# Twelve of the 22 row chunks of a down projection as seven block products in place of eight, placed inside the up stage

## The chip, the cores and the metric

The kernel runs on one core of a Trainium2 chip. The metric is the time of one execution on the device in microseconds. TensorE (PE in the profile, PEld for its weight loads) multiplies; VectorE (DVE) and ScalarE (ACT) do the elementwise work; GpSimd (POOL) does little here; SyncE (SP) issues nearly all transfers. The engines run side by side, each through its own instructions in order, and wait for each other through semaphores.

## What is computed

Two encoder layers on 512 tokens of width 1024. Each adds to the residual `x` a mixture of three attention branches, and then a feed-forward part. Only the second is touched:

```python
def conv_ffn(h, w_up, conv_w, conv_b, w_down):      # D_FF = 2816, D_MODEL = 1024
    u = h @ w_up
    C = u.shape[-1]
    u = lax.conv_general_dilated(u, conv_w[:, None, :].astype(u.dtype), window_strides=(1,),
                                 padding=((CONV_W // 2, CONV_W // 2),),
                                 dimension_numbers=('NWC', 'WIO', 'NWC'),
                                 feature_group_count=C) + conv_b
    a, g = jnp.split(u, 2, axis=-1)
    return (jax.nn.gelu(g) * a) @ w_down

for l in range(DEPTH):                              # DEPTH = 2
    ...
    h = rmsnorm(x, norm2_g[l])
    x = x + conv_ffn(h, w_up[l], conv_w[l], conv_b[l], w_down[l])
return rmsnorm(x, final_g)
```

## The kernel before

Everything is held transposed: features on the 128 partitions, the 512 tokens along a row. `x` is eight tiles of 128x512 (`self.x[k]`, two of which carry other names in the trace). A product of full float32 accuracy is made of three matmuls in the format fp32r: weight and data are each split into a high part (a rounded copy, ACT, L153) and a low part (the remainder, one subtraction on DVE, L154), and `mm3` (L162 to L169) adds high times high, high weight times low data, low weight times high data into one PSUM bank.

Weights: `self.specs` lists every block of weights in the order of use. `fetch` loads each into one of three buffers `raw` by a DMA on SP's queue and splits it into `whi` and `wlo`, three buffers each. `weights(spec)`, called just ahead of a block's matmuls, lets the loads run to two blocks ahead and the splits too; a pair of split buffers is free again when the matmuls of the block three places earlier are done.

The up stage (`do_up`, `conv`) walks 22 value chunks f and their 22 gate chunks in turns: 24 matmuls of 512 columns make one chunk in one of eight PSUM banks; DVE scales it by the norm (`u`), ACT and DVE apply the three taps of the convolution (`c`, L906 to L908), a gate chunk goes through Gelu and is multiplied with its value chunk, and the product is split into the pair `ff` of its chunk. The down stage (`do_down`) then has two groups of four output tiles. A group walks the 22 chunks of `ff` in pieces of 8, 8 and 6: for each piece and each of the four output tiles one block of weights, 24, 24 and 18 matmuls, into that tile's bank (`ps_g`). After the last piece DVE adds the bank to `x[k]`, once for each tile (L944; in three tiles of the last layer L941 and L978), and the next norm begins. The last three tiles of the last layer are multiplied in `finish`, two of them in halves of 256 tokens.

The order on PE and SP is the order of the code (`manual_schedule`). On ACT and DVE a scheduler sets the order when the program is built, from priorities: a split runs 300 places ahead (`PRIO`). Engines are held apart by semaphores that count their instructions; a PSUM tile is watched as a whole.

Of the kernel before, what the change touches and what calls it, by code (L numbers as in the profile page):

```python
# [10 lines left out]
F32 = mybir.dt.float32  # L11
# [3 lines left out]
ALU = mybir.AluOpType  # L15
# [21 lines left out]
LAT = (0, 1, 2, 3)  # L37
ATTN, ATTN_PRIO = ("mr", "ms", "mt", "mp", "ns", "nt", "np", "gs", "gt", "gp"), 100
RAWB, WB, GZB, PRIO = 3, 3, 5, 300
ROWS = (slice(0, 64), slice(64, 128))  # L40
HALVES = (ROWS, ROWS[::-1])

# [17 lines left out]
class Trunk:  # L60
# [5 lines left out]
    def __init__(self, ctx, tc, d):  # L66
        self.tc, self.nc, self.d, self.ctx = tc, tc.nc, d, ctx
        nc = self.nc
        self.small = ctx.enter_context(tc.tile_pool(name="small", bufs=1))
        self.const = ctx.enter_context(tc.tile_pool(name="const", bufs=1))  # L70
        self.wp = ctx.enter_context(tc.tile_pool(name="wp", bufs=1))
        self.psum = ctx.enter_context(tc.tile_pool(name="psum", bufs=1, space=bass.MemoryType.PSUM))
        self.groups, self.turn = {}, {}
        c = self.const
        x0 = c.tile([P, S + NPC], F32, name="x0")
        self.x = [x0[:, :S]] + [c.tile([P, S], F32, name=f"x{k}") for k in range(1, KD)]
        self.par = [x0[:, S:], self.small.tile([P, NPC], F32, name="par1")]
        self.early = c.tile([P, P], F32, tag="acc", name="early")
        nc.vector.memset(self.early, 1.0)
        self.idf = c.tile([P, P], F32, name="idf")  # L80
        make_identity(nc, self.idf)
        cst = self.small.tile([P, 6], F32, name="cst")
        self.neghalf, self.ones = cst[:, 0:4], cst[:, 4:5]
        nc.vector.memset(self.neghalf, -0.5)
        nc.vector.memset(self.ones, 1.0)
        self.warm = cst[:, 5:6]
        nc.scalar.activation(self.warm, self.ones, AF.Exp)
        self.specs, self.raws, self.parts, self.used = [], [], [], 0
        self.plans = [self.schedule(l) for l in range(L)]
        for s, W in self.plans:  # L90
            self.specs += [w for item in s for w in W.get(item, ())]
        nc.sync.dma_start(x0[:, :S + PC_CW], d["x0"])
        self.fetch(1, 0)
        for k in range(1, 5):
            nc.sync.dma_start(self.x[k], d["xT"][k * P:(k + 1) * P, :])
            self.fetch(min(k + 1, 3), 0)
        self.gmask = self.small.tile([P, 3 * P], BF16, name="gmask")
# [12 lines left out]


    def fetch(self, n_raw, n_split):
        nc = self.nc
        while len(self.raws) < min(n_raw, len(self.specs)):
            w, r0, nk, c0, cw = self.specs[len(self.raws)]
            raw = self.wp.tile([P, 1024], F32, tag="raw", name="raw", bufs=RAWB)
            for q, a, b in ((nc.sync, 0, cw),) if self.raws else ((nc.scalar, 0, P), (nc.sync, P, cw)):
                q.dma_start(raw[:, :nk * cw].rearrange("p (k c) -> p k c", c=cw)[:, :, a:b],
                            w[r0:r0 + nk * P, c0 + a:c0 + b].rearrange("(k p) c -> p k c", p=P))
            self.raws.append(raw)  # L120
        while len(self.parts) < min(n_split, len(self.raws)):
            i = len(self.parts)
            w, r0, nk, c0, cw = self.specs[i]
            hi = self.wp.tile([P, 1024], F32R, tag="whi", name="whi", bufs=WB)
            lo = self.wp.tile([P, 1024], F32R, tag="wlo", name="wlo", bufs=WB)
            if cw == 64:
                both = hi[:].rearrange("p (k c) -> p k c", c=P)
                with self.tc.high_priority(offset=PRIO if self.prio else 0):
                    self.split(both[:, :, 0:64], both[:, :, 64:P],
                               self.raws[i][:, :nk * cw].rearrange("p (k c) -> p k c", c=cw))  # L130
                self.parts.append((both, both))
                continue
            with self.tc.high_priority(offset=PRIO if self.prio else 0):
                if i:
                    self.split(hi[:, :nk * cw], lo[:, :nk * cw], self.raws[i][:, :nk * cw])
                else:
                    for cp, c in ((nc.vector.tensor_copy, slice(0, P)), (nc.scalar.copy, slice(P, 4 * P))):
                        cp(hi[:, c], self.raws[i][:, c])
            self.parts.append(tuple(t[:, :nk * cw].rearrange("p (k c) -> p k c", c=cw) for t in (hi, lo)))

    def weights(self, spec):
        i = self.used
        assert self.specs[i][1:] == spec[1:]
        self.fetch(i + RAWB, i + WB)
        self.used += 1
        wh, wl = self.parts[i]
        return [(wh[:, k, :], wl[:, k, :]) for k in range(spec[2])]


    def split(self, hi, lo, src, scale=None):  # L150
# [123 lines left out]
    def schedule(self, l):  # L274
# [30 lines left out]
        W["up"] = halves(d["w_up"][l], [f * P for f in ups[:4]])  # L305
        for f in ups[4:]:
            W["up", f] = [(d["w_up"][l], 0, KD, f * P, P)]
        for g in range(2):
            W["down", g] = [(d["w_down"][l], k0 * P, nk, (4 * g + m) * P, P)
                            for k0, nk in ((0, 8), (8, 8), (16, 6)) for m in range(4)]  # L310

        gate = iter([("gate", b, m) for b in (1, 0, 2) for m in range(8)]).__next__
        s = ["mla_open", "lat", "qr", "lat4", "rs_q", "kr", gate(), "rs_k", ("qn", 0), ("v", 0), ("v", 1), "rb_k"]
# [16 lines left out]
            s += [gate(), ("br", 2, m)]  # L330
        s += [("br", 2, 7)]
        s += ["out"] + [("out", m) for m in range(4, KD)]
        s += ["up"] + [("up", f) for f in ups[4:]]
        s += [("down", 0), ("down", 1)]
        return s, W

# [551 lines left out]
    def do_up(self, fi=None):  # L888
        if fi is None:
            self.banks(g=[2, 3, 4, 5], r=[6], d=[7, 0, 1, 2, 3, 4, 5, 6])  # L890
            self.fps, self.fp = self.open("ff")
            self.ff = []
            ups = [0, NF, 1, NF + 1]
            conv = lambda *js: [self.conv(ups[j], self.gbank[j]) for j in js]
            self.group(self.W["up"], self.h, {(0, 1): lambda: (self.norm_sums(), self.norm_spread()), (1, 0): lambda: conv(0), (1, 1): lambda: conv(1),
                                              (1, 2): lambda: conv(2), (1, 3): lambda: conv(3)})
        else:
            self.conv(fi, self.dense(self.spec(), self.h))

    def conv(self, fi, ps):  # L900
        nc, pr = self.nc, self.pr
        u = self.fp.tile([P, S], F32, tag="u", name="u", bufs=2)
        self.mul(u, ps, self.rb)
        c = self.fp.tile([P, S], F32, tag="c", name="c", bufs=3)
        cw = pr[:, PC_CW + 3 * fi:PC_CW + 3 * fi + 3]
        nc.scalar.activation(c, u, AF.Identity, bias=pr[:, PC_CB + fi:PC_CB + fi + 1], scale=cw[:, 1:2])  # L906
        nc.vector.scalar_tensor_tensor(c[:, 1:], u[:, :S - 1], cw[:, 0:1], c[:, 1:], ALU.mult, ALU.add)
        nc.vector.scalar_tensor_tensor(c[:, :S - 1], u[:, 1:], cw[:, 2:3], c[:, :S - 1], ALU.mult, ALU.add)  # L908
        if fi < NF:
            self.ca = c  # L910
            return
        nc.scalar.activation(c, c, AF.Gelu_apprx_tanh)
        self.mul(self.ca, self.ca, c)
        f = fi - NF
        pair = [self.fp.tile([P, S], F32R, tag=f"f{n}{f}", name="ff") for n in "hl"]
        self.split(*pair, self.ca)
        self.ff.append(pair)

    def do_down(self, g):
        nc = self.nc  # L920
# [12 lines left out]
        for i, spec in enumerate(self.W["down", g]):  # L933
            m, k0, nk = i % 4, spec[1] // P, spec[2]
            if last and (g, k0, m) == (1, 16, 1):
                self.finish([self.weights(sp) for sp in self.W["down", 1][i:]], self.ff[k0:k0 + nk])
                break
            tail = last and g == 1 and m > 0
            self.mm3(ps[m], self.weights(spec), self.ff[k0:k0 + nk], k0 == 0, k0 == (8 if tail else 16))
            if tail and k0 == 8:  # L940
                nc.vector.tensor_add(self.x[4 + m], self.x[4 + m], ps[m])  # L941
            if k0 == 16:
                k = 4 * g + m
# [6 lines left out]
                else:  # L950
                    self.norm_piece(k, self.par[self.l + 1][:, PC_G1:PC_G1 + 8])
        if g == 1:
            self.fps.close()

    def finish(self, sts, mv):
# [7 lines left out]
        for k in range(5, KD):  # L963
            self.xg.append(self.const.tile([P, S], F32, tag=f"hh{k}", name="xg"))
        sq = [self.const.tile([P, S], F32, tag=f"hl{k}", name="sq") for k in range(5, KD)]
        outs = [self.fp.tile([P, 2, S], F32, tag="o", name="o", bufs=3) for _ in range(3)]
        outs.append([self.const.tile([P, S], F32, tag=t, name="o") for t in ("hl3", "hl4")])
        rts = self.small.tile([P, 4], F32, tag="rt", name="rts", bufs=3)
        eps = self.small.tile([P, 4], F32, tag="ms", name="eps", bufs=2)
# [6 lines left out]
        def add(m, ts):  # L976
            x = self.x[4 + m][:, ts]
            nc.vector.tensor_add(x, x, ps[m][:, ts])  # L978
            nc.scalar.activation(sq[m - 1][:, ts], x, AF.Square)
# [139 lines left out]
```

## Time and profile before

| | us |
|---|---|
| median of three timed runs | 1689.85 (1689.12 to 1689.95) |
| the profiled execution | 1688.89 |
| its span, first to last instruction | 1687.1 |
| PE busy | 1678.7, 8466 matmuls |
| PE weight loads busy | 1388.2 |
| DVE busy | 1119.5 |
| ACT busy | 832.5 |

A row of the timeline gives the start and the duration of an instruction, or of several alike (x3), both in microseconds; in a group row the numbers behind the first bar are the busy time and the mean duration in nanoseconds. Matmuls run into each other: each row's duration holds the time in which its last results drain while the next matmul already runs. What a matmul costs in a full stream is therefore the distance between starts, not its duration. The same holds, less strongly, for DVE and ACT.

### The profile page before, as it was taken

Reading aid. Unit: us, or ns where it says so; the run is one execution under the profiler, and the core shown is the slowest. Engines: PE = TensorE matmul, PEld = TensorE weight load, DVE = VectorE, ACT = ScalarE, POOL = GpSimd, SP = SyncE. Lnnn points to the kernel's source line nnn. Section 1 sums busy time; section 2 is a strip of 40 time slices with the busy share of each in tenths; the row PEclk is TensorE's granted clock in tenths of the full one; section 3 lists DMA queues with packets and bytes.
Section 4 is the critical chain, followed back from the end, with each engine's and each line's share of the span. In section 5 each row is a group of like instructions: output and inputs, shape, how many; then the busy total and the mean of one; then the engine's idle time right before and its main releaser. Section 6 shows DMA issues by size and latency. Waiting matters only on the chain.

```text
span 1687.1 us, 22130 instructions
## 1 busy us (share of the span) xinstructions
PE 1678.7 (100%) x8466; PEld 1388.2 (82%) x8466; DVE 1119.5 (66%) x1845; ACT 832.5 (49%) x1461; POOL 51.8 (3%) x107
## 2 busy tenths in 40 slices
PE   9999999999999999999999999999999999999998
PEld 8888888888888888888887888888888888888887
DVE  7677866787558777734367687667866587777234
ACT  7664445775435444423266554457744444444232
POOL 1110000000000000000011100000000000000000
PEclk9999999999999999999999999999999999999999
DMA  6233323222334333323233323332223333333231
GB/s 186 67 98 90 89 77 88 81 63 81 108 87 118 99 91 99 100 87 103 79 97 82 91 82 94 82 88 63 69 83 106 106 102 99 100 99 91 86 106 69
DMA packets 289401, 155.44 MB, mean 92 GB/s; under 512 B 8880, under 2 KB 285376, under 8 KB 289296
## 3 DMA queue, kind: packets, MB, share of 16 engines
q1 hardware_dynamic: 286752, 148.88, 30.8%
q0 software_dynamic: 2256, 4.83, 0.9%
q8 instruction: 66, 1.08, 0.3%
q14 instruction: 39, 0.32, 0.1%
q10 hardware_dynamic: 288, 0.33, 0.1%
HBM read 151.89 MB, written 2.10 MB: 91 GB/s over the span
## 4 chain that ended last, share of the span: by engine, by line
PE 97%; DVE 2%; ACT 0%; issue 0%; ACTq 0%
PE ps_ring L167 13%; PE ps_ring L168 12%; PE ps_ring L169 12%; PE ps_d L169 11%; PE ps_d L168 11%; PE ps_d L167 11%; PE ps_g L168 7%; PE ps_g L167 7%; PE ps_g L169 7%; PE ps_ring L247 2%; PE ps_ring L234 1%; PE ps_g L267 1%; PE ps_ring L702 1%; PE ps_ring L857 1%; PE ps_ring L856 1%; DVE wlo L154 1%
## 5 line engine op out<-in xcount | busy, mean ns | idle before, releaser
L153 ACT CAST whi<-raw 128x1024 fp32r<-128x1024 f32 (+4 forms) x339 | 301.0, 888 | 589.0 <-PE ps_g L168 192.3
L154 DVE TENSOR_TENSOR wlo<-raw,whi 128x1024 fp32r<-128x1024 f32 (+4 forms) x337 | 344.4, 1022 | 183.7 <-ACT whi L153 183.1
L169 PE MATMUL ps_d<-hh,wlo 128*128 128x512 f32 x685 | 266.5, 389 | 0.0
L168 PE MATMUL ps_d<-hl,whi 128*128 128x512 f32 x685 | 266.5, 389 | 0.0
L167 PE MATMUL ps_d<-hh,whi 128*128 128x512 f32 x685 | 266.5, 389 | 0.0
L167 PE MATMUL ps_ring<-hh,whi 128*128 128x512 f32 x600 | 235.3, 392 | 0.5 <-DVE pt L674 0.5
L169 PE MATMUL ps_ring<-hh,wlo 128*128 128x512 f32 x600 | 233.8, 390 | 0.0
L168 PE MATMUL ps_ring<-hl,whi 128*128 128x512 f32 x600 | 233.6, 389 | 0.0
L168 PEld LDWEIGHTS ps_d<-hl,whi 128*128 128x128 f32 x685 | 128.6, 188 | 27.0
L167 PEld LDWEIGHTS ps_d<-hh,whi 128*128 128x128 f32 x685 | 128.6, 188 | 26.8
L169 PEld LDWEIGHTS ps_d<-hh,wlo 128*128 128x128 f32 x685 | 128.6, 188 | 26.6 <-DVE wlo L154 0.2
L167 PEld LDWEIGHTS ps_ring<-hh,whi 128*128 128x128 f32 x600 | 112.7, 188 | 24.4 <-DVE pt L674 0.9
L169 PEld LDWEIGHTS ps_ring<-hh,wlo 128*128 128x128 f32 x600 | 112.6, 188 | 23.8
L168 PEld LDWEIGHTS ps_ring<-hl,whi 128*128 128x128 f32 x600 | 112.6, 188 | 23.1
L168 PE MATMUL ps_g<-ff,whi 128*128 128x512 f32 x334 | 129.9, 389 | 0.0
L169 PE MATMUL ps_g<-ff,wlo 128*128 128x512 f32 x334 | 129.9, 389 | 0.0
L167 PE MATMUL ps_g<-ff,whi 128*128 128x512 f32 x334 | 129.9, 389 | 0.0
L160 DVE TENSOR_TENSOR u<-ps_d,rb 128x512 f32<-128x512 f32 x80 | 55.2, 690 | 63.2 <-PE ps_d L169 63.2
L160 DVE TENSOR_TENSOR gz<-ps_ring,rb 128x512 f32<-128x512 f32 x44 | 30.4, 690 | 78.1 <-PE ps_ring L169 78.1
L167 PEld LDWEIGHTS ps_g<-ff,whi 128*128 128x128 f32 x334 | 62.7, 188 | 13.1
L169 PEld LDWEIGHTS ps_g<-ff,wlo 128*128 128x128 f32 x334 | 62.7, 188 | 13.1
L168 PEld LDWEIGHTS ps_g<-ff,whi 128*128 128x128 f32 x334 | 62.7, 188 | 12.9
(331 smaller groups left out, 2859.5 us busy)
## 6 DMA issues: line engine op xcount, KB each, us to landing
raw<-in_w_in_dram SPq DMA_DIRECT2D x86, 512.0 KB, 3.9
raw<-in_w_up_dram SPq DMA_DIRECT2D x80, 512.0 KB, 3.8
raw<-in_w_down_dram SPq DMA_DIRECT2D x32, 512.0 KB, 3.9
raw<-in_w_down_dram SPq DMA_DIRECT2D x16, 384.0 KB, 3.4
raw<-in_w_in_dram SPq DMA_DIRECT2D x17, 256.0 KB, 2.9
raw<-in_w_br_mla_dram SPq DMA_DIRECT2D x16, 256.0 KB, 2.7
raw<-in_w_br_na_dram SPq DMA_DIRECT2D x16, 256.0 KB, 2.7
raw<-in_w_br_gqa_dram SPq DMA_DIRECT2D x16, 256.0 KB, 2.8
```

Source lines behind the costliest of these rows:

```text
L153: nc.scalar.copy(hi, src)
L154: nc.vector.tensor_sub(lo, src, r32(hi))
L160: self.nc.vector.tensor_tensor(out, a, b, ALU.mult)
L167: mm(ps, sh, mh, start=first and k == 0, stop=False)
L168: mm(ps, sh, ml, start=False, stop=False)
L169: mm(ps, sl, mh, start=False, stop=last and k == n - 1)
L234: self.nc.tensor.transpose(out[i][:, n * 64:n * 64 + 64], block[q], self.idf[q, q])
L247: self.nc.tensor.matmul(out, st[a], mv[b], start=first and t == 0, stop=last and t == 2)
L267: self.nc.tensor.matmul(self.gbank[j], w[:, j * P:(j + 1) * P], m, start=n + t == 0, stop=False)
L702: nc.tensor.matmul(pq[:, qs], self.vs[p][:, ch, j, :], pm[:].rearrange("p (k c) -> p k c", c=P)[:, ks], start=i == 0 and m == 0, stop=i == ...
L856: nc.tensor.matmul(po, self.gvs[:, k0 + kb, g, :], ph, start=kb == 0, stop=False)
L857: nc.tensor.matmul(po, self.gvs[:, k0 + kb, g, :], pl, start=False, stop=kb == nk - 1)
```

## The change

Per layer, the first 12 of the 22 chunks (6 pairs of chunks, `NP = 6`) are multiplied by the scheme of seven block products in place of eight (Strassen's, in Winograd's form). A unit takes two neighbouring output tiles (`m`, `m + 1`), the even and the odd chunk of each pair, and the two halves of the tokens: 2 x 2 blocks of weights, 2 x 2 blocks of data. Seven combinations of weight blocks (`ORDER`, each 128x768: six blocks of 128 columns) meet seven combinations of data blocks (`B11` to `T4`, each 256 tokens wide). Each of the seven is an item of 6 x 3 = 18 matmuls of 256 columns. There are four units in each layer, so 28 items and 504 matmuls.

- Data: `sum_operands` puts the gated product of a pair of chunks into `prod` and makes its seven high and low parts (`ft`), 256 tokens each.
- Weights: `load_sum` loads four tiles of 128x768 for a unit (`V11`, `V21`, `V22`, `V12`; up to seven items ahead); `prepare_sum` makes `S1`, `S2`, `S4` one after the other in one tile, and `S3`, by four additions on DVE, and splits each of the seven.
- Products: `do_sum` writes the items of a unit into two PSUM banks, each used in two halves, and after each item adds the finished half to, or subtracts it from, `x` at once (L1009, 256 wide; L1012 for the seventh, 512 wide), at a priority 400 places ahead (`EVAC`).
- Place: the four units stand in the up stage, after chunk f = 12 and before f = 13. The remaining ten chunks go through `do_down` as before, in pieces of 4 and 6.

```diff
+NP, AHEAD, EVAC = 6, 7, 400
+ORDER = ("V11", "S1", "V12", "S2", "S4", "V22", "S3")
+B11, B21, B22, T1, T3, T2, T4 = range(7)
...
     def fetch(self, n_raw, n_split):
+        while len(self.raws) < len(self.specs):
+            spec = self.specs[len(self.raws)]
+            if len(self.raws) >= n_raw + (AHEAD - RAWB if spec[0] == "sum" else 0):
+                break
+            self.raws[len(self.raws)] = self.load_sum(*spec[1:]) if spec[0] == "sum" else self.load(*spec)
...
+    def prepare_sum(self, hi, lo, j, unit):
+        add, name = self.nc.vector.tensor_add, ORDER[j]
+        if j == 0:
+            unit["S3"] = self.fa.tile([P, NP * P], F32, tag="s3", name="s3")
+        elif j == 1:
+            unit["S1"] = unit["S2"] = unit["S4"] = self.fa.tile([P, NP * P], F32, tag="s1", name="s1")
+            add(unit["S1"], unit["V21"], unit["V22"])
+        elif name in ("S2", "S4"):
+            add(unit[name], unit[name], unit["V11" if name == "S2" else "V12"])
+        self.split(hi[:, :NP * P], lo[:, :NP * P], unit[name])
+        if j == 0:
+            add(unit["S3"], unit["V11"], unit["V21"])
+        return tuple(t[:, :NP * P].rearrange("p (k c) -> p k c", c=P) for t in (hi, lo))
...
+        for m in range(0, KD, 2):
+            unit = {"w": d["w_down"][l], "m": m}
+            W["sum", m] = [("sum", j, unit) for j in range(7)]
         for g in range(2):
             W["down", g] = [(d["w_down"][l], k0 * P, nk, (4 * g + m) * P, P)
-                            for k0, nk in ((0, 8), (8, 8), (16, 6)) for m in range(4)]
+                            for k0, nk in ((2 * NP, 4), (16, 6)) for m in range(4)]
...
-        s += ["up"] + [("up", f) for f in ups[4:]]
+        n = 2 * (2 * NP + 1)
+        s += ["up"] + [("up", f) for f in ups[4:n]] + [("sum", m) for m in range(0, KD, 2)] + [("up", f) for f in ups[n:]]
...
+    def sum_operands(self, f, c):
+        nc, (i, e) = self.nc, divmod(f, 2)
+        half = lambda t, a, n: t[:, a * 256:(a + n) * 256]
...
+        hi, lo = self.ff[i]
+        self.mul(half(self.prod, 2 * e, 2), self.ca, c)
+        if e == 0:
+            self.split(half(hi, B11, 1), half(lo, B11, 1), half(self.prod, 0, 1))
+            return
+        self.split(half(hi, B21, 2), half(lo, B21, 2), half(self.prod, 2, 2))
+        b = self.prod[:].rearrange("p (n c) -> p n c", c=256)
+        a, t = (self.fa.tile([P, 2 * 256], F32, tag="tt", name="tt", bufs=2) for _ in range(2))
+        nc.vector.tensor_tensor(a[:].rearrange("p (n c) -> p n c", c=256), b[:, 0::3],
+                                b[:, 1:2].to_broadcast([P, 2, 256]), ALU.subtract)
+        self.split(half(hi, T1, 2), half(lo, T1, 2), a)
+        nc.vector.scalar_tensor_tensor(half(t, 0, 1), half(a, 0, 1), -1.0, b[:, 3], ALU.mult, ALU.subtract)
+        nc.vector.scalar_tensor_tensor(half(t, 1, 1), half(t, 0, 1), -1.0, b[:, 2], ALU.mult, ALU.subtract)
+        self.split(half(hi, T2, 2), half(lo, T2, 2), t)
+
+    def do_sum(self, m):
+        nc, mm = self.nc, self.nc.tensor.matmul
+        banks = [self.bank("d") for _ in range(2)]
+        first, second = slice(0, 256), slice(256, 512)
+        x1, x2 = self.x[m], self.x[m + 1]
+        steps = ((B11, 0, first, x1[:, first], 1), (T1, 1, first, x2[:, second], -1), (B21, 0, second, x1[:, first], 1),
+                 (T2, 0, first, x1[:, second], 1), (B22, 1, first, x1[:, second], 1), (T4, 1, second, x2[:, first], -1),
+                 (T3, 0, first, x2, -1))
+        for j, (spec, (operand, b, part, x, sign)) in enumerate(zip(self.W["sum", m], steps)):
+            ps = banks[b][:, part]
+            c = slice(operand * 256, operand * 256 + 256)
+            for i, (wh, wl) in enumerate(self.weights(spec)):
+                hi, lo = (t[:, c] for t in self.ff[i])
+                mm(ps, wh, hi, start=j < 2 and i == 0, stop=False, skip_group_check=True)
+                mm(ps, wh, lo, start=False, stop=False, skip_group_check=True)
+                mm(ps, wl, hi, start=False, stop=i == NP - 1, skip_group_check=True)
+            with self.tc.high_priority(offset=EVAC):
+                if j < 6:
+                    nc.vector.tensor_tensor(x, x, ps, ALU.add if sign > 0 else ALU.subtract)
+                else:
+                    both = x.rearrange("p (n c) -> p n c", c=256)
+                    nc.vector.tensor_tensor(both, both, ps.rearrange("p (n c) -> p n c", n=1).to_broadcast([P, 2, 256]),
+                                            ALU.subtract)
```

**Where the instructions stand: PE.** In the rows below a name's number is that of a tile, the second number pair the size of the output, and the brackets name the engines whose count the instruction waits for. Before, in the down stage of the first layer, PE goes from the block of one output tile (`ps_g_6745`) to that of the next (`ps_g_6746`):

```order
L168 MATMUL ps_g_6745<-ff_5621,whi_6703 128x512
L169 MATMUL ps_g_6745<-ff_5620,wlo_6704 128x512
L167 MATMUL ps_g_6746<-ff_5086,whi_6751 128x512 [waits Activation_49]
L168 MATMUL ps_g_6746<-ff_5087,whi_6751 128x512
L169 MATMUL ps_g_6746<-ff_5086,wlo_6752 128x512 [waits DVE_49]
```

Of the change, the same engine in the second unit of the first layer, from item 2 (counted from 0) to item 3, which both write the tile `ps_d_6260`, item 2 its second half and item 3 its first:

```order
L1004 MATMUL ps_d_6260<-ft_5903,whi_6262 128x256
L1005 MATMUL ps_d_6260<-ft_5904,whi_6262 128x256
L1006 MATMUL ps_d_6260<-ft_5903,wlo_6263 128x256
L1004 MATMUL ps_d_6260<-ft_5089,whi_6291 128x256 [waits DVE_49,Activation_49]
L1005 MATMUL ps_d_6260<-ft_5090,whi_6291 128x256
L1006 MATMUL ps_d_6260<-ft_5089,wlo_6292 128x256
```

Before, the first matmul of a block waits for its own weights alone, and writes another bank than the one before it. Now the first matmul of item 3 also waits for DVE. Counted through in the built program, the count that it waits for is that of the addition to `x2_69` of item 2, the second of the two that read `ps_d_6260` up to there. Item 5 waits in the same way for the addition of item 4 (both in the other bank), in each of the eight units.

**Where the instructions stand: DVE.** Before, at this place of the up stage, DVE splits the weights and applies the convolution:

```order
L154 TENSOR_TENSOR ff_6021<-c_5977,ff_6020 128x512 [waits Activation_49]
L907 SCALAR_TENSOR_TENSOR c_6057<-u_6055,x0_67,c_6057 128x511 [waits Activation_49]
L908 SCALAR_TENSOR_TENSOR c_6057<-u_6055,x0_67,c_6057 128x511 [waits DVE_49]
L160 TENSOR_TENSOR u_6092<-ps_d_6067,rb_4996 128x512 [waits PE_49]
L154 TENSOR_TENSOR wlo_6107<-raw_6104,whi_6106 128x1024 [waits DMAHW7_49,Activation_49]
```

Of the change, DVE in the second unit, from the split for item 3 to the addition of item 4 (L1009 additions to `x`, L192 splits, L173 `S4`, L171 and L176 `S1` and `S3` of the third unit):

```order
L192 TENSOR_TENSOR wlo_6292<-s1_6237,whi_6291 128x768 [waits Activation_49]
L173 TENSOR_TENSOR s1_6237<-s1_6237,raw_6162 128x768 [waits DVE_49]
L1009 TENSOR_TENSOR x3_70<-x3_70,ps_d_6261 128x256 [waits PE_49]
L192 TENSOR_TENSOR wlo_6316<-s1_6237,whi_6315 128x768 [waits Activation_49]
L1009 TENSOR_TENSOR x2_69<-x2_69,ps_d_6260 128x256 [waits PE_49]
L192 TENSOR_TENSOR wlo_6342<-own_6112,whi_6341 128x768 [waits Activation_49]
L171 TENSOR_TENSOR s1_6414<-raw_6287,own_6289 128x768 [waits DMAHW5_49,DMAHW4_49,DVE_49]
L1009 TENSOR_TENSOR x2_69<-x2_69,ps_d_6260 128x256 [waits PE_49]
L192 TENSOR_TENSOR wlo_6365<-s3_6212,whi_6364 128x768 [waits Activation_49]
L176 TENSOR_TENSOR s3_6389<-own_6285,raw_6287 128x768 [waits DMAHW3_49,DVE_49]
L1009 TENSOR_TENSOR x2_69<-x2_69,ps_d_6261 128x256 [waits PE_49]
```

The additions to `x` of items 1, 2, 3 and 4 now stand between splits and sums of weights. The second (item 2) has one split ahead of it, the last (item 4) a split and a sum.

More of the change, by code (lines that the diff above doesn't have):

```diff
@@ L87, in __init__ @@
         nc.scalar.activation(self.warm, self.ones, AF.Exp)
-        self.specs, self.raws, self.parts, self.used = [], [], [], 0
+        self.specs, self.raws, self.parts, self.used = [], {}, [], 0
         self.plans = [self.schedule(l) for l in range(L)]
@@ L112, in fetch @@
     def fetch(self, n_raw, n_split):
[L113 to L120, printed above, removed]
+        while len(self.raws) < len(self.specs):
[3 more added lines that the diff above has]
+            self.raws[len(self.raws)] = self.load_sum(*spec[1:]) if spec[0] == "sum" else self.load(*spec)
@@ L121, in fetch @@
         while len(self.parts) < min(n_split, len(self.raws)):
             i = len(self.parts)
[L123 to L132, printed above, removed]
+            hi, lo = (self.wp.tile([P, 1024], F32R, tag=t, name=t, bufs=WB) for t in ("whi", "wlo"))
@@ L133, in fetch @@
             with self.tc.high_priority(offset=PRIO if self.prio else 0):
-                if i:
-                    self.split(hi[:, :nk * cw], lo[:, :nk * cw], self.raws[i][:, :nk * cw])
-                else:
-                    for cp, c in ((nc.vector.tensor_copy, slice(0, P)), (nc.scalar.copy, slice(P, 4 * P))):
-                        cp(hi[:, c], self.raws[i][:, c])
-            self.parts.append(tuple(t[:, :nk * cw].rearrange("p (k c) -> p k c", c=cw) for t in (hi, lo)))
+                if self.specs[i][0] == "sum":
+                    self.parts.append(self.prepare_sum(hi, lo, *self.specs[i][1:]))
+                else:
+                    self.parts.append(self.prepare(hi, lo, self.raws[i], *self.specs[i]))
@@ new lines, in load, with prepare @@
+    def load(self, w, r0, nk, c0, cw):
+        nc = self.nc
+        raw = self.wp.tile([P, 1024], F32, tag="raw", name="raw", bufs=RAWB)
+        for q, a, b in ((nc.sync, 0, cw),) if self.raws else ((nc.scalar, 0, P), (nc.sync, P, cw)):
+            q.dma_start(raw[:, :nk * cw].rearrange("p (k c) -> p k c", c=cw)[:, :, a:b],
+                        w[r0:r0 + nk * P, c0 + a:c0 + b].rearrange("(k p) c -> p k c", p=P))
+        return raw
+    def prepare(self, hi, lo, raw, w, r0, nk, c0, cw):
+        nc = self.nc
+        view = lambda t: t[:, :nk * cw].rearrange("p (k c) -> p k c", c=cw)
+        if cw == 64:
+            both = hi[:].rearrange("p (k c) -> p k c", c=P)
+            self.split(both[:, :, 0:64], both[:, :, 64:P], view(raw))
+            return both, both
+        if self.parts:
+            self.split(hi[:, :nk * cw], lo[:, :nk * cw], raw[:, :nk * cw])
+        else:
+            for cp, c in ((nc.vector.tensor_copy, slice(0, P)), (nc.scalar.copy, slice(P, 4 * P))):
+                cp(hi[:, c], raw[:, c])
+        return view(hi), view(lo)
@@ new lines, in load_sum @@
+    def load_sum(self, j, unit):
+        for name in {0: ("V11", "V21", "V22"), 2: ("V12",)}.get(j, ()):
+            m, e = unit["m"] + int(name[1]) - 1, int(name[2]) - 1
+            if name in ("V11", "V22"):
+                t = self.fa.tile([P, NP * P], F32, tag="own", name="own", bufs=4)
+            else:
+                t = self.wp.tile([P, 1024], F32, tag="raw", name="raw", bufs=RAWB)
+            unit[name] = t[:, :NP * P]
+            rows = unit["w"][0:2 * NP * P, m * P:(m + 1) * P].rearrange("(i e p) c -> e p i c", e=2, p=P)
+            self.nc.sync.dma_start(unit[name].rearrange("p (i c) -> p i c", c=P), rows[e])
@@ L146, in weights @@
         wh, wl = self.parts[i]
-        return [(wh[:, k, :], wl[:, k, :]) for k in range(spec[2])]
+        return [(wh[:, k, :], wl[:, k, :]) for k in range(NP if spec[0] == "sum" else spec[2])]
     def split(self, hi, lo, src, scale=None):
@@ L891, in do_up @@
             self.fps, self.fp = self.open("ff")
+            self.fas, self.fa = self.open("fa")
             self.ff = []
@@ L912, in conv @@
         nc.scalar.activation(c, c, AF.Gelu_apprx_tanh)
+        f = fi - NF
+        if f < 2 * NP:
+            self.sum_operands(f, c)
+            return
         self.mul(self.ca, self.ca, c)
-        f = fi - NF
-        pair = [self.fp.tile([P, S], F32R, tag=f"f{n}{f}", name="ff") for n in "hl"]
+        pool = self.fp if f == 2 * NP else self.fb
+        pair = [pool.tile([P, S], F32R, tag=f"f{n}{f}", name="ff") for n in "hl"]
         self.split(*pair, self.ca)
         self.ff.append(pair)
+    def sum_operands(self, f, c):
+        nc, (i, e) = self.nc, divmod(f, 2)
+        half = lambda t, a, n: t[:, a * 256:(a + n) * 256]
+        if e == 0:
+            self.prod = self.fa.tile([P, 4 * 256], F32, tag="prod", name="prod")
+            self.ff.append([self.fa.tile([P, 7 * 256], F32R, tag=f"t{n}{i}", name="ft") for n in "hl"])
+        hi, lo = self.ff[i]
+        self.mul(half(self.prod, 2 * e, 2), self.ca, c)
+        if e == 0:
+            self.split(half(hi, B11, 1), half(lo, B11, 1), half(self.prod, 0, 1))
+            return
+        self.split(half(hi, B21, 2), half(lo, B21, 2), half(self.prod, 2, 2))
[7 more added lines that the diff above has]
+        self.split(half(hi, T2, 2), half(lo, T2, 2), t)
@@ new lines, in do_sum @@
+    def do_sum(self, m):
[17 more added lines that the diff above has]
+                    nc.vector.tensor_tensor(x, x, ps, ALU.add if sign > 0 else ALU.subtract)
+                else:
+                    both = x.rearrange("p (n c) -> p n c", c=256)
+                    nc.vector.tensor_tensor(both, both, ps.rearrange("p (n c) -> p n c", n=1).to_broadcast([P, 2, 256]),
+                                            ALU.subtract)
+        if m == KD - 2:
+            self.ff = self.ff[NP:]
+            self.fas.close()
+            self.fbs, self.fb = self.open("fb")
@@ L935, in do_down @@
             if last and (g, k0, m) == (1, 16, 1):
-                self.finish([self.weights(sp) for sp in self.W["down", 1][i:]], self.ff[k0:k0 + nk])
+                self.finish([self.weights(sp) for sp in self.W["down", 1][i:]], self.ff[k0 - 2 * NP:])
                 break
             tail = last and g == 1 and m > 0
-            self.mm3(ps[m], self.weights(spec), self.ff[k0:k0 + nk], k0 == 0, k0 == (8 if tail else 16))
-            if tail and k0 == 8:
+            self.mm3(ps[m], self.weights(spec), self.ff[k0 - 2 * NP:k0 - 2 * NP + nk], k0 < 16, tail or k0 == 16)
+            if tail and k0 < 16:
                 nc.vector.tensor_add(self.x[4 + m], self.x[4 + m], ps[m])
@@ L952, in do_down @@
         if g == 1:
+            self.fbs.close()
             self.fps.close()
@@ L965, in finish @@
         sq = [self.const.tile([P, S], F32, tag=f"hl{k}", name="sq") for k in range(5, KD)]
-        outs = [self.fp.tile([P, 2, S], F32, tag="o", name="o", bufs=3) for _ in range(3)]
+        outs = [self.fb.tile([P, 2, S], F32, tag="o", name="o", bufs=3) for _ in range(3)]
         outs.append([self.const.tile([P, S], F32, tag=t, name="o") for t in ("hl3", "hl4")])
```

## The prediction

> **What bounds the kernel now.** I read the page first: the span, the busy times, the clock and the chain that ended last.
>
> ```profile
> span 1687.1 us, 22130 instructions
> PE 1678.7 (100%) x8466; PEld 1388.2 (82%) x8466; DVE 1119.5 (66%) x1845; ACT 832.5 (49%) x1461; POOL 51.8 (3%) x107
> ...
> PEclk9999999999999999999999999999999999999999
> ...
> PE 97%; DVE 2%; ACT 0%; issue 0%; ACTq 0%
> ```
>
> PE is never without work and its clock is never cut; 97% of the chain is PE's own. So the kernel's time is the number of matmuls times the distance of their starts, and a gain can only be fewer or cheaper matmuls; a loss is anything that makes PE wait. Next I looked at the two stages that the change touches, the up stage and the down stage of the second layer, in the view by stretches of time (length, then busy time and instructions of PE, PEld, DVE, ACT, POOL, then clock, DMA share, GB/s):
>
> ```profile
> 1320.00:1559.00 239.00, 239.00 (x1058) 197.77 (x1057) 173.44 (x222) 106.09 (x135) 3.58 (x4) 1.00 0.35 103
> 1559.00:1664.00 105.00, 105.00 (x465) 86.95 (x464) 31.88 (x35) 26.91 (x32) 0.00 (x0) 1.00 0.30 85
> ```
>
> DVE is busy 73% of the up stage and 30% of the down stage: both engines beside PE have room. The price of a matmul is read from the timeline of PE near the end, where 512 and 256 columns stand side by side:
>
> ```profile
> 1639.78 0.39 PE L167 MATMUL ps_g<-ff,whi 128*128 128x512 f32 x1
> ...
> 1664.04 0.39 PE L169 MATMUL ps_g<-ff,wlo 128*128 128x512 f32 x1
> ...
> 1668.34 0.28 PE L167 MATMUL ps_z<-ff,whi 128*128 128x256 f32 x1
> ...
> 1670.38 0.28 PE L169 MATMUL ps_z<-ff,wlo 128*128 128x256 f32 x1
> 1670.50 0.28 PE L167 MATMUL ps_z<-ff,whi 128*128 128x256 f32 x1
> ```
>
> From 1639.78 to 1664.04 lie 107 steps: 24.26 / 107 = 0.2267 us for 512 columns. From 1668.34 to 1670.50 lie 18 steps, one output tile's half: 2.16 / 18 = 0.120 us for 256 columns. Half the columns cost 53%, since 0.1067 us per 256 columns and a fixed 0.0133 us per matmul fit both.
>
> **Term 1: the matmuls.** Removed in each layer: 12 chunks x 8 tiles x 3 = 288 matmuls of 512 columns, 288 x 0.2267 = 65.3 us. Added: 4 units x 7 items x 18 = 504 of 256 columns, 504 x 0.120 = 60.5 us. That is -4.8 us a layer, **-9.6 us** in all. Of the eighth that the scheme saves, a good third goes into the fixed part of 216 more matmuls. Each matmul also loads its weights, and this takes longer than the step of 0.120 us:
>
> ```profile
> L169 PEld LDWEIGHTS ps_g<-ff,wlo 128*128 128x128 f32 x334 | 62.7, 188 | 13.1
> ```
>
> The 18 steps above ran at 0.120 us all the same, so loads overlap each other and the matmuls, as long as nothing stops them. The Trainium skill ("TensorE: Matmul & The Clock Gate", Back-to-back issue gap) puts the fixed part of a warm matmul at 2.5 ns rather than 13.3; by it term 1 would be 288 x 215.8 ns - 504 x 109.2 ns = 7.1 us a layer, -14.2 us in all. The rows here contradict it, for these fp32r matmuls at least, and the rows decide.
>
> **Term 2: two new waits in each unit.** Item 3 writes the bank whose other half DVE is just to read for item 2, and waits until that addition is done; so does item 5 behind item 4. PE is in order, so all matmuls stand behind the waiting one. An addition of 256 columns from PSUM stands in the trace, right behind the 18 matmuls above, and so do a split with the operation behind it and the copy that feeds it:
>
> ```profile
> 1664.24 0.84 ACT L153 CAST whi<-raw 128x768 fp32r<-128x768 f32 x1 [3.24 <-PE ps_g L168]
> 1664.46 0.69 DVE L944 TENSOR_TENSOR x<-x,ps_g 128x512 f32<-128x512 f32 x1 [2.48 <-PE ps_g L169]
> 1665.11 0.96 DVE L154 TENSOR_TENSOR wlo<-raw,whi 128x768 fp32r<-128x768 f32 x1
> 1665.98 0.68 DVE L186 TENSOR_TENSOR acc<-acc,sq 128x512 f32<-128x512 f32 x1
> 1670.70 0.42 DVE L978 TENSOR_TENSOR x<-x,ps_z 128x256 f32<-128x256 f32 x1
> ```
>
> What it costs PE to be released by DVE is seen where a matmul of the neighbourhood attention waited for a bank that DVE read:
>
> ```profile
> 161.71 1.88 DVE L674 SCALAR_TENSOR_TENSOR pt<-ps_ring,tm 128x512 f32<-128x512 f32 x3
> L674 DVE SCALAR_TENSOR_TENSOR pt<-ps_ring,tm 128x512 f32<-128x512 f32 x32 | 20.0, 680 | 0.0
> 162.44 0.50 PE L167 MATMUL ps_ring<-h,whi 128*128 128x512 f32 x1 [0.20 <-DVE pt L674]
> 162.78 0.39 PE L168 MATMUL ps_ring<-h,whi 128*128 128x512 f32 x1
> 162.44 0.19 PEld L167 LDWEIGHTS ps_ring<-h,whi 128*128 128x128 f32 x1 [0.33 <-DVE pt L674]
> ```
>
> The first of the three ends at 161.71 + 0.68 = 162.39; PE goes on at 162.44, 0.05 later. The weight load starts with the matmul, not before it, and the next matmul follows after 0.34 us in place of 0.227: 0.11 us of the load is now bare.
>
> So the least that one wait costs, with S the start of the last matmul of an item: it ends at S + 0.28 (1670.38 to 1670.66), the addition starts 0.04 later (1670.70) and takes 0.42, S + 0.74; PE goes on at S + 0.79. It would have gone on at S + 0.12. With the bare load: 0.79 - 0.12 + 0.11 = **0.78 us**.
>
> DVE is in order too, and the additions stand behind splits and sums. I walk the second unit by the order shown above, with these rows:
>
> ```profile
> L154 DVE TENSOR_TENSOR wlo<-raw,whi 128x768 fp32r<-128x768 f32 x18 | 17.3, 962 | 40.5 <-ACT whi L153 40.5
> L153 ACT CAST whi<-raw 128x768 fp32r<-128x768 f32 x18 | 15.1, 838 | 68.9 <-PE ps_g L168 68.8
> L661 DVE TENSOR_TENSOR tm<-nmask,tb 128x768 f32<-128x768 f32 x16 | 15.0, 947 | 0.0
> ```
>
> A sum of two 128x768 tiles is not in the trace of before; the nearest row of the same operation and size takes 0.95 us (L661), and I use it. An independent operation starts 0.09 before the end of the one ahead (1665.11 + 0.96 to 1665.98), a dependent one 0.03 after it (ACT 1664.24 + 0.84 to DVE 1665.11).
>
> - Second wait. Item 3's last matmul starts at S. The copy of the next split needs only the buffer of the last `whi`, free one matmul earlier (1664.24 against 1664.46 shows it): it runs from S + 0.20 to S + 1.04, the split from S + 1.07 to S + 2.03, the dependent sum `S3` from S + 2.06, and DVE is free at S + 2.92. Item 4 ends one item later, so its addition was due at S + 2.16 + 0.32 = S + 2.48: 0.44 late, a wait of 0.78 + 0.44 = **1.22 us**.
> - First wait. By the same steps the sum `S4` holds item 1's addition until S + 2.92, which is 0.76 after item 1's last start. The next split's copy needs this sum (done 0.85 after that start, copied by 1.72), the split runs from 1.75, DVE is free at 2.62, and item 2's addition was due at 2.48: 0.14 late, **0.92 us**.
> - The two inner units pay 2.14 us each. In the last there is no further unit's sum behind item 3: 0.92 + 0.78. In the first the wait behind item 2 meets no late split (0.78), and behind item 3 stands a split of `ff`, 512 wide, in place of the sum: about 1.0. A layer: 2 x 2.14 + 1.70 + 1.78 = 7.8 us; both layers **+15.5 us**, 16 waits of 0.97 us on average.
>
> **Costed at nothing.** DVE's work in a unit: seven splits, four sums, six additions of 256 and one of 512, in steps of 0.87, 0.86, 0.33 and 0.60: 12.1 us, against 15.1 us of matmuls and 2 us of waits. It fits, and the splits run two items ahead, 4.3 us against 0.84 + 0.96: PE should not wait for weights. If it did, each late split would cost as much as it is late. The extra data parts (per two chunks one subtraction and two 256-wide ones, three splits of 512 for one, about 2.6 us on DVE per 21.8 us of matmuls) lift DVE in the up stage from 73% to about 85%, still hidden. Loads: four transfers of 384 KB per unit in 17 us are 92 GB/s, where the up stage moves 103. ACT adds less than DVE and has more room. The down stage keeps 10 chunks, whose pieces of 4 need a split of 512 per 2.7 us: hidden. SP's queue only waits for buffers freed several items before.
>
> **Sum.** -9.6 + 15.5 = +5.9 us. The profiled execution took 1688.89 us, so 1694.8; the median shown is 0.96 above it, so I predict **1695.8 us**.
>
> **The rivals.**
> - *The waits cost less than the matmuls save (faster).* With the waits gone, the time is 1689.85 - 9.6 = 1680.3. For it: additions are put first by priority, and PE has 0.16 us of drain anyway. The point where it wins by 0.2% (3.4 us) is (9.6 - 3.4) / 16 = 0.39 us a wait, less than the addition's own 0.42 us. Only if the bank's other half could be written without waiting would that happen, and the built program has the wait. 10%.
> - *The floor everywhere (no change).* If the scheduler's order does not delay the additions, 16 x 0.78 = 12.5 us, net +2.9: 1692.7. The walk's delays rest on 0.1 to 0.4 us differences, so 16%. The rule of the skill on the 2.5 ns belongs here as a mechanism: 256-column matmuls spaced 0.109 us would give 1689.85 - 14.2 + 15.5 = 1691.1. The 18 measured steps speak against it: 2%.
> - *DVE becomes the bound (slower still).* If each addition finds a 768 split just begun, the wait is 0.78 + 0.87 = 1.65 us, 26.4 in all: 1706.7. For it: DVE is at 70% in a unit and in order. Against it: the splits have two items of slack. Half the waits so gives 1701. 14%.
> - *It does not save matmul time.* The counts are certain (504 for 288) and both steps measured; included in the cases above.
>
> **How the numbers follow.** Forecast (1693.3 to 1700): 58%. Range: below, two microseconds under the floor case and most of the rule's case; above, past the case of half the waits doubled: 1690.5 to 1702.5. A measurement of this kernel can tell about 0.2% (3.4 us) from no change; by it faster 10%, same 18%, slower 72%.
>
> **What would show it.** In the changed profile: matmuls of L1004 to L1006 at 0.120 us between starts; PE idle just before L1004 sixteen times, released by L1009 on DVE, and the first matmul after each longer by 0.11; the stretch of 28 items 68.2 us long (60.5 + 7.8); no PE waits for `whi` or `wlo`; the clock still uncut. Wrong would be: fewer than 16 such waits, steps other than 0.120 us, PE waiting for L192 or a DMA, or a stage outside the units that grows.

## The result, and the profile after

| us | before | with the change |
|---|---|---|
| median of five runs each | 1689.12 | 1697.13 (1696.87 to 1697.30) |
| ratio to before | | 1.0047, 95% interval 1.0032 to 1.0062 |
| profiled execution | 1688.89 | 1697.28 |
| its span | 1687.1 | 1695.5 |

The change makes the kernel slower by 8.0 us; the forecast was 1695.8 us, 5.95 over the median of the first three runs. The page of the changed kernel, with the lines that answer to those of before:

```profile
span 1695.5 us, 23333 instructions
PE 1673.0 (99%) x8898; PEld 1401.6 (83%) x8898; DVE 1216.3 (72%) x2033; ACT 868.1 (51%) x1525; POOL 52.9 (3%) x107
...
PEclk9999999999999999999999999999999999999999
...
PE 95%; DVE 3%; ACT 1%; POOLq 0%; issue 0%; POOL 0%; ACTq 0%
```

PE is busy 5.7 us less and the span is 8.4 us longer: PE sat idle for 8.4 us of the span before and for 22.5 us now, and its share of the chain went from 97% to 95%. The view of waits of the changed kernel says where the 14.1 us more are (engine, line, whom it waited for, microseconds in total, times, longest):

```profile
PE ps_d L1004 <- DVE x L1009: 6.9, 8, 1.1
PE ps_d L1004 <- ACT whi L191: 6.8, 8, 0.9
...
PE ps_d L207 <- DVE wlo L192: 0.4, 1, 0.4
```

Sixteen waits, all at the first matmul of an item of 18, and one of 0.4 us in the up stage. The stretches of the second layer (length, busy time and count of PE, PEld, DVE, ACT, POOL, then clock, DMA share, GB/s): the up stage to the units, the four units, and the rest of the up stage with the beginning of the down stage:

```profile
1318.50:1463.40 144.90, 144.51 (x639) 119.35 (x639) 114.76 (x166) 69.36 (x95) 3.58 (x4) 1.00 0.38 109
1463.40:1532.60 69.20, 62.35 (x506) 60.95 (x505) 53.27 (x75) 25.48 (x31) 0.00 (x0) 1.00 0.28 77
1532.60:1640.00 107.40, 107.40 (x476) 88.90 (x475) 74.17 (x96) 46.48 (x60) 0.00 (x0) 1.00 0.31 92
```

PE idles for 6.85 us in the units and for 0.4 us ahead of them. The clock is uncut, and DVE is busy 77% of the units. The second unit of the first layer in the timeline of DVE, ACT and PE, from `S4` to item 5 (rows sorted by engine):

```profile
644.46 0.96 DVE L173 TENSOR_TENSOR s<-s,raw 128x768 f32<-128x768 f32 x1
645.34 0.41 DVE L1009 TENSOR_TENSOR x<-x,ps_d 128x256 f32<-128x256 f32 x1
646.39 0.96 DVE L192 TENSOR_TENSOR wlo<-s,whi 128x768 fp32r<-128x768 f32 x1 [0.65 <-ACT whi L191]
647.27 0.41 DVE L1009 TENSOR_TENSOR x<-x,ps_d 128x256 f32<-128x256 f32 x1
...
651.05 0.96 DVE L192 TENSOR_TENSOR wlo<-s,whi 128x768 fp32r<-128x768 f32 x1 [0.38 <-ACT whi L191]
652.04 0.96 DVE L176 TENSOR_TENSOR s<-own,raw 128x768 f32<-128x768 f32 x1
652.92 0.41 DVE L1009 TENSOR_TENSOR x<-x,ps_d 128x256 f32<-128x256 f32 x1
```
```profile
642.60 0.83 ACT L191 CAST whi<-s 128x768 fp32r<-128x768 f32 x1 [1.37 <-DVE wlo L192]
645.53 0.83 ACT L191 CAST whi<-s 128x768 fp32r<-128x768 f32 x1 [2.09 <-DVE s L173]
646.92 0.83 ACT L191 CAST whi<-own 128x768 fp32r<-128x768 f32 x1 [0.56 <-PE ps_d L1005]
```
```profile
646.68 0.28 PE L1006 MATMUL ps_d<-ft,wlo 128*128 128x256 f32 x1
647.83 0.36 PE L1004 MATMUL ps_d<-ft,whi 128*128 128x256 f32 x1 [0.87 <-ACT whi L191]
648.02 0.28 PE L1005 MATMUL ps_d<-ft,whi 128*128 128x256 f32 x1
648.14 0.28 PE L1006 MATMUL ps_d<-ft,wlo 128*128 128x256 f32 x1
```

Item 2 ends at 646.96, its addition runs from 647.27 to 647.68, and item 3 begins at 647.83. From the start of the last matmul to that of the next it is 1.15 us in place of 0.12, and one more step is 0.19 long. All 16 counted so, from the timeline of PE: 8.7 us in each layer, **17.4 us**. The matmuls save 9.6, which leaves +7.8 of the 8.0 us.

The name behind the first wait is misleading: eight times the page says that PE waited for the copy `whi`. That copy (646.92 to 647.75) is of item 5's weights, and the row above it, right behind the sum `S4`, is of item 4's; item 3's own began at 642.60 and was done at 643.43, four microseconds before. The profile names the semaphore event that came last before the start. That it was the addition is settled by the experiments.

### The profile page after: what moved, and what is told of

Its sections match the earlier page's. It is cut to its first block, busy times and chain, and to the rows that moved or that the text cites. A ratio compares the mean times of both kernels' runs of the same rounds, so it can differ in the third digit from the quotient of the medians.

```text
span 1695.5 us, 23333 instructions
## 1 busy us (share of the span) xinstructions
PE 1673.0 (99%) x8898; PEld 1401.6 (83%) x8898; DVE 1216.3 (72%) x2033; ACT 868.1 (51%) x1525; POOL 52.9 (3%) x107
## 3 DMA queue, kind: packets, MB, share of 16 engines
q8 instruction: 70, 1.15, 0.3%
## 4 chain that ended last, share of the span: by engine, by line
PE 95%; DVE 3%; ACT 1%; POOLq 0%; issue 0%; POOL 0%; ACTq 0%
PE ps_ring L205 12%; PE ps_ring L206 12%; PE ps_ring L207 12%; PE ps_d L207 11%; PE ps_d L205 11%; PE ps_d L206 11%; PE ps_g L207 4%; PE ps_g L205 4%; PE ps_g L206 4%; PE ps_d L1004 2%; PE ps_d L1005 2%; PE ps_d L1006 2%; PE ps_ring L285 2%; PE ps_ring L272 1%; ACT whi L191 1%; DVE wlo L192 1%
## 5 line engine op out<-in xcount | busy, mean ns | idle before, releaser
L191 ACT CAST whi<-raw 128x1024 fp32r<-128x1024 f32 (+3 forms) x331 | 284.1, 858 | 470.8 <-PE ps_ring L206 151.9
L192 DVE TENSOR_TENSOR wlo<-raw,whi 128x1024 fp32r<-128x1024 f32 (+3 forms) x329 | 323.5, 983 | 80.6 <-ACT whi L191 79.9
L1004 PE MATMUL ps_d<-ft,whi 128*128 128x256 f32 x336 | 96.2, 286 | 13.7 <-DVE x L1009 6.9
L1005 PE MATMUL ps_d<-ft,whi 128*128 128x256 f32 x336 | 95.0, 283 | 0.0
L1006 PE MATMUL ps_d<-ft,wlo 128*128 128x256 f32 x336 | 95.0, 283 | 0.0
L1004 PEld LDWEIGHTS ps_d<-ft,whi 128*128 128x128 f32 x336 | 64.3, 191 | 16.6 <-ACT whi L191 13.0
L192 DVE TENSOR_TENSOR pl<-ps_ring,ph 128x512 fp32r<-128x512 f32 x104 | 65.5, 680 | 1.6 <-ACT ph L191 1.6
L1005 PEld LDWEIGHTS ps_d<-ft,whi 128*128 128x128 f32 x336 | 64.4, 192 | 0.1
```

The costliest lines, as they stand in the source:

```text
L191: nc.scalar.copy(hi, src)
L192: nc.vector.tensor_sub(lo, src, r32(hi))
L1004: mm(ps, wh, hi, start=j < 2 and i == 0, stop=False, skip_group_check=True)
L1005: mm(ps, wh, lo, start=False, stop=False, skip_group_check=True)
L1006: mm(ps, wl, hi, start=False, stop=i == NP - 1, skip_group_check=True)
```

## The experiments

**A third bank.** All the work stays; only the two products that stand alone move to a bank of their own.

```diff
-        banks = [self.bank("d") for _ in range(2)]
+        banks = [self.bank("d") for _ in range(3)]
...
-        steps = ((B11, 0, first, x1[:, first], 1), (T1, 1, first, x2[:, second], -1), (B21, 0, second, x1[:, first], 1),
-                 (T2, 0, first, x1[:, second], 1), (B22, 1, first, x1[:, second], 1), (T4, 1, second, x2[:, first], -1),
+        steps = ((B11, 0, first, x1[:, first], 1), (T1, 1, first, x2[:, second], -1), (B21, 2, first, x1[:, first], 1),
+                 (T2, 0, first, x1[:, second], 1), (B22, 1, first, x1[:, second], 1), (T4, 2, second, x2[:, first], -1),
...
-                mm(ps, wh, hi, start=j < 2 and i == 0, stop=False, skip_group_check=True)
+                mm(ps, wh, hi, start=j < 3 and i == 0, stop=False, skip_group_check=True)
```

> Items 2 and 5 of each unit (the two products that stand alone) write a third PSUM bank, so no item follows an item in the same bank; the matmuls, splits, sums and additions are the same in number and size. My theory (16 waits behind additions to x, 17.4 us by the trace of the change): all 16 go, the 28 items of a layer take 60.5 us, and the time is 1697.1 - 17.4 = 1679.7 us, 9.4 us faster than the kernel before. Rival 1 (DVE with its splits and sums is the bound of a unit, and the waits only show it): PE then waits for wlo or whi in place of x, and at most a third of the 17.4 us is saved, 1691 us or more. Rival 2 (256-column matmuls are dearer than 0.120 us in this stage): the starts stay further apart than 0.120 us and the time stays over 1690.

Measured: **1679.77 us**, 0.9943 of before (0.9930 to 0.9955). The four units of the first layer in the view by stretches, and where PE leaves them in its timeline:

```profile
624.00:684.50 60.50, 60.50 (x506) 60.49 (x505) 52.34 (x75) 25.37 (x31) 0.73 (x1) 1.00 0.30 83
```
```profile
624.01 0.28 PE L1004 MATMUL ps_d<-ft,whi 128*128 128x256 f32 x1
...
684.37 0.28 PE L1006 MATMUL ps_d<-ft,wlo 128*128 128x256 f32 x1
684.49 0.40 PE L205 MATMUL ps_d<-hh,whi 128*128 128x512 f32 x1
```

504 matmuls take 60.48 us, 0.120 each, without one wait; DVE does the same 52 us of work in them, now 87% of the stretch, and delays nothing. Both rivals fall, and this version is faster than the kernel before by 9.4 us and than the change by 17.4.

**One of the two waits.** Only item 5 gets the third bank.

```diff
-        banks = [self.bank("d") for _ in range(2)]
+        banks = [self.bank("d") for _ in range(3)]
...
-                 (T2, 0, first, x1[:, second], 1), (B22, 1, first, x1[:, second], 1), (T4, 1, second, x2[:, first], -1),
+                 (T2, 0, first, x1[:, second], 1), (B22, 1, first, x1[:, second], 1), (T4, 2, second, x2[:, first], -1),
...
-                mm(ps, wh, hi, start=j < 2 and i == 0, stop=False, skip_group_check=True)
+                mm(ps, wh, hi, start=j in (0, 1, 5) and i == 0, stop=False, skip_group_check=True)
```

> Only item 5 has a bank of its own; item 3 still follows item 2 in the same bank. My theory: the eight waits behind item 4 go, in the trace of the change 0.86, 1.15, 1.15 and 0.77 us late starts in a layer with the step of 0.12 us taken off counted with 0.07 each for the bare weight load (1.02, 1.34, 1.34, 0.84 us; 9.1 us in both layers), and the eight behind item 2 stay as they are: 1697.1 - 9.1 = 1688.0 us. Rival 1 (DVE is the bound): the other wait of the unit grows by what this one loses, and the time stays within 3 us of 1697.

Measured: 1688.01 us (0.9990 of before, 0.9981 to 0.9999), 9.1 us less than the change. (The late starts without the weight load are 0.95, 1.27, 1.27 and 0.76 us in the trace of the change, not 0.86, 1.15, 1.15 and 0.77; the figures in the brackets, from which 9.1 comes, agree with it.) The price is that of each wait by itself; the other eight stay as they were:

```profile
PE ps_d L1004 <- ACT whi L191: 5.3, 6, 0.9
PE ps_d L1004 <- DVE x L1009: 1.2, 2, 0.6
```

**No sums of weights.**

```diff
-            add(unit["S1"], unit["V21"], unit["V22"])
+            unit["S1"] = unit["S2"] = unit["S4"] = unit["V21"]
-        elif name in ("S2", "S4"):
-            add(unit[name], unit[name], unit["V11" if name == "S2" else "V12"])
...
-            add(unit["S3"], unit["V11"], unit["V21"])
+            unit["S3"] = unit["V21"]
```

> The four sums of weight blocks of a unit (S1 to S4) are left out and the tile V21 stands in for them, so the output is not that of the reference; matmuls, splits, additions to x and both waits of a unit stay. My theory (each wait has a floor of 0.83 us, and what lies above it comes from a sum on DVE ahead of the addition): the 16 waits stay but fall to 0.83 us each, 13.3 us in place of 17.4; the time is 1697.1 - 4.1 = 1693 us. Rival 1 (DVE's load is the bound): with a quarter of DVE's work in a unit gone the waits nearly vanish, 1683 us or less. Rival 3 (the price is that of the bank, the order on DVE plays no part): nothing changes, 1697.

Measured: 1693.74 us (1.0027 of before, 1.0018 to 1.0037), 3.4 us less than the change where 4.1 were expected. Here the page names DVE for all 16:

```profile
PE ps_d L1002 <- DVE x L1007: 9.9, 16, 0.7
```

In the first layer seven of the eight gaps between starts are 0.88 or 0.89 us, the floor of 0.76 over the step plus 0.07; the first is 1.00. Neither rival's time came (1683 or less, or 1697). So about a fifth of the 17.4 us comes from sums on DVE that stand ahead of an addition, and four fifths are the addition itself with what lies around it.

**The wait alone on its matmul.** This one is on a number in the prediction that was off: PE goes on 0.15 us after the addition's end (647.68 to 647.83), not 0.05.

```diff
-        banks = [self.bank("d") for _ in range(2)]
+        banks = [self.bank("d") for _ in range(3)]
...
+                if i == 0 and j in (3, 5):
+                    mm(banks[2][:, 0:64], wh, hi[:, 0:64], start=True, stop=True)
```

> A matmul of 64 columns into a bank of its own stands ahead of items 3 and 5 and takes the wait for the weights' copy, so that the first matmul of the item waits for the addition alone and no longer for two engines. It tests why PE went on 0.15 us after the end of the addition, where I had taken 0.05. If a second wait on the same matmul costs the 0.10 us, PE goes on 0.05 us after the addition here; 16 x 0.10 us less, 1695.5 us (the extra matmul lies in the wait). If the 0.15 us belong to the addition (a short operation, its result late), it stays 0.15 and the time is 1697.

Measured: 1696.78 us, in one run. The addition on DVE and the matmuls on PE at the same place as above:

```profile
648.02 0.42 DVE L1011 TENSOR_TENSOR x<-x,ps_d 128x256 f32<-128x256 f32 x1
```
```profile
647.42 0.28 PE L1008 MATMUL ps_d<-ft,wlo 128*128 128x256 f32 x1
647.54 0.20 PE L1005 MATMUL ps_d<-ft,whi 128*128 128x64 f32 x1
648.49 0.39 PE L1006 MATMUL ps_d<-ft,whi 128*128 128x256 f32 x1 [0.75 <-DVE x L1011]
648.71 0.28 PE L1007 MATMUL ps_d<-ft,whi 128*128 128x256 f32 x1
```

The addition ends at 648.44 and PE goes on at 648.49: 0.05 us (0.05 or 0.06 at all 16 places), and the page now names the addition. So PE goes on 0.09 us later where its matmul waits for two engines at once. The trace of the change shows what fills this time: at each of the 16 places the queue of PE's weight loads (PEldq) holds an instruction that only waits, `EVENT_SEMAPHORE`. It begins 0.04 us after the addition's end and takes 0.05, and the matmul follows 0.055 us behind it. In this run those 16 are gone; the eight others stand in both traces and delay no matmul. The rows of the two traces, the change first (count, duration in ns, first and last start):

```profile
L1004 PEldq EVENT_SEMAPHORE  x24: 51/51/51, 626.2 to 1528.0; - x24
```
```profile
L1006 PEldq EVENT_SEMAPHORE  x8: 51/51/51, 627.0 to 1517.9; - x8
```

Of the 1.6 us expected, the two traces show 0.8 (against steps of 0.120 us, PE falls behind by 17.2 us in the units of the change and by 16.5 here) and the time 0.35, which one run cannot tell from nothing. One reason is in the rows: the step behind the wait is 0.22 us here and 0.19 in the change, so a part of the weight load that had been hidden is bare again.

**Two banks, another order.** The same two banks, but the products ordered so that the banks alternate.

```diff
-ORDER = ("V11", "S1", "V12", "S2", "S4", "V22", "S3")
+ORDER = ("V11", "S1", "S2", "S4", "V12", "V22", "S3")
...
-        steps = ((B11, 0, first, x1[:, first], 1), (T1, 1, first, x2[:, second], -1), (B21, 0, second, x1[:, first], 1),
-                 (T2, 0, first, x1[:, second], 1), (B22, 1, first, x1[:, second], 1), (T4, 1, second, x2[:, first], -1),
+        steps = ((B11, 0, first, x1[:, first], 1), (T1, 1, first, x2[:, second], -1), (T2, 0, first, x1[:, second], 1),
+                 (B22, 1, first, x1[:, second], 1), (B21, 0, second, x1[:, first], 1), (T4, 1, second, x2[:, first], -1),
                  (T3, 0, first, x2, -1))
```

> Two banks as in the change, but the seven products in another order (B11, T1, T2, B22, B21, T4, T3): the banks now alternate, so no item follows an item in its own bank. S1, S2 and S4 are then needed by three items in a row, which ties DVE's sums closer. My theory (what costs is that an item follows another in the same bank, not how many banks a unit has): the 16 waits go, as with the third bank, and the time is 1679.7 us, up to 1682 if the closer row of sums makes PE wait for a split once in the first unit of a layer. Rival (two banks are too few for this scheme in any order): waits behind L1009 stay, 1690 us or more.

Measured: 1683.18 us (0.9965 of before, 0.9952 to 0.9977). No wait behind an addition is left:

```profile
PE ps_d L1006 <- DVE wlo L192: 1.4, 2, 0.7
...
PE ps_d L1004 <- ACT whi L191: 0.3, 2, 0.2
```

What costs is that an item follows another in the same bank, not the number of banks. This version is 3.4 us slower than the one with the third bank, and 1.2 us over the upper end expected. In each layer PE falls behind by 1.4 us at the item of `S4`, in the second unit and not in the first. The rows of DVE there, in the first layer:

```profile
643.81 0.42 DVE L1009 TENSOR_TENSOR x<-x,ps_d 128x256 f32<-128x256 f32 x1 [0.83 <-PE ps_d L1006]
644.15 0.95 DVE L173 TENSOR_TENSOR s<-s,raw 128x768 f32<-128x768 f32 x1
645.97 0.42 DVE L1009 TENSOR_TENSOR x<-x,ps_d 128x256 f32<-128x256 f32 x1 [0.87 <-PE ps_d L1006]
646.31 0.95 DVE L192 TENSOR_TENSOR wlo<-s,whi 128x768 fp32r<-128x768 f32 x1
```

The sum `S4` stands behind an addition for which DVE waits 0.83 us, and its split then ends at 647.26, after PE has come to the item. That makes 2.8 of the 3.4 us; the rest was not traced.

**Halves without the scheme.** The kernel before, its first 12 chunks in halves of 256 tokens, with all eight block products.

```diff
-            self.mm3(ps[m], self.weights(spec), self.ff[k0:k0 + nk], k0 == 0, k0 == (8 if tail else 16))
+            st, mv, end = self.weights(spec), self.ff[k0:k0 + nk], k0 == (8 if tail else 16)
+            for k in range(nk):
+                (sh, sl), (mh, ml) = st[k], mv[k]
+                for t, (w, d) in enumerate(((sh, mh), (sh, ml), (sl, mh))):
+                    for h in ((slice(0, 256), slice(256, 512)) if k0 + k < 12 else (slice(0, 512),)):
+                        nc.tensor.matmul(ps[m][:, h], w, d[:, h], start=k0 + k + t + h.start == 0,
+                                         stop=end and k == nk - 1 and t == 2, skip_group_check=True)
```

> The kernel before, with the first 12 chunks of the down projection multiplied as before (eight block products) but in halves of 256 tokens: 576 matmuls of 256 columns a layer in place of 288 of 512, nothing else changed. My theory (256 columns cost 0.120 us, 512 cost 0.2267): 576 x 0.120 - 288 x 0.2267 = 3.8 us a layer, 7.7 in all, 1689.15 + 7.7 = 1696.8 us. Rival (the fixed part is 2.5 ns in place of 13.3, as the Trainium skill, TensorE: Matmul & The Clock Gate, Back-to-back issue gap, has it, and the rest of the distance goes with the columns): 288 x 2.5 ns x 2 layers = 1.4 us, 1690.6 us.

Measured: 1697.24 us (1.0047 of before, 1.0032 to 1.0062): +8.2 us where 7.7 were worked out, far from the 1.4 of the rival. In the trace the halves start 0.120 us apart, so cutting each product in two costs here what it costs in the scheme. The Trainium skill's 2.5 ns (TensorE: Matmul & The Clock Gate, Back-to-back issue gap), which that section calls the isolated gap of a single matmul, does not hold for these matmuls, for which the runs show 13.3.

## Why the prediction was right

- *PE is the bound, and the matmuls save 9.6 us.* Right. With the waits gone, 60.48 us a layer were measured where 60.5 were worked out, and the kernel is 9.4 us faster than before.
- *Two waits in each unit, behind the additions of items 2 and 4.* Right, in number and place. Without both the time falls by 17.4 us, without the second by 9.1.
- *A wait costs 0.78 us at least, 0.97 on average, 15.5 us in all.* This is the term that was mis-sized: 0.83 and 1.09 us, 17.4 in all, and a layer's 28 items take 69.1 us where 68.2 were forecast. Two steps of it failed, each for about half of the 1.9 us.
  - The floor. PE's release was put at 0.05 us from a row of the attention, whose matmul waits for one engine; it is 0.15 where the matmul waits for two. Against that the weight load is bare for 0.07 us and not 0.11. The two errors partly offset each other, which was luck.
  - DVE's order. The copy behind an item starts 0.24 us after the item's last matmul, not 0.20, and a sum takes 0.02 more than was put down. So the addition of item 4 begins 0.55 us after the item in place of 0.48. At item 2 the copy that depends on a sum comes in addition: it was put 0.03 us behind the sum and comes 0.11 behind (645.42 to 645.53), and the addition begins 0.31 us after the item in place of 0.18.
- *DVE does not become the bound.* Right: it is busy 87% of the units in the version without waits and PE never waits for it. That the additions were put ahead by priority made no difference: built with a priority of 0, the program is the same, instruction for instruction.
- *Loads, data parts and the shorter down stage cost nothing.* Right to about half a microsecond. One wait of 0.4 us for a split, at the beginning of the second up stage, is new; the traces of the other versions of the scheme do not have it. DVE is busy 79% of the up stage ahead of the units, where about 85% were put down.
- *The rival of the Trainium skill's 2.5 ns* is settled by the halves without the scheme.

That the bank is watched as a whole is the framework's doing, but not its whim: the Trainium skill (PSUM — Partial Sum Buffer, Terms) calls it a collision when two engines are in one bank and quadrant at once, an error in which colliding reads return wrong data. No run here lets PE write a bank that DVE reads, so this was not tried.

## What to carry to other kernels

A scheme that saves an eighth of the multiplications saves less than that where each product is cut smaller: here a good third of the gain went into the fixed part of each matmul, and 9.6 us were left to spend. Before such a gain is booked, look at each place where an item writes a PSUM bank that another engine is just about to read: every such place cost PE about a microsecond, and the 16 together nearly twice the 9.6 us. A third bank removed this cost whole, and an order in which the banks alternate was 3.4 us short of that. And where a page names who was waited for, see if that work was the waiting instruction's own; when it was for another item, the cause is the other of its waits.

## What had not been expected of the hardware

- A matmul that waits for two engines went on 0.15 us after the addition was done, at all 16 places, with an instruction of 0.05 us that only waits ahead of it. With the other wait taken by an earlier matmul that instruction was gone, and PE went on after 0.05 to 0.06 us. Where no matmul stood waiting, such instructions cost nothing: 22 of them stand in the units of the version with the third bank, which ran at 0.120 us throughout.
- Weight loads of 0.19 us ran behind each other at 0.120 us for 60.48 us on end (busy 60.49 of 60.50 us), and cost nothing as long as no wait broke the row.
